# The S5 recurrence of a transformer block, computed in blocks of four time steps instead of step by step

## The chip, the core and the metric

The kernel runs on one core of one Trainium2 chip. Five engines work side by side from queues of their own: TensorE (PE; its weight loads are shown as PEld), VectorE (DVE), ScalarE (ACT), GpSimd (POOL) and SyncE (SP), which here issues the DMAs. They wait for each other through semaphores. TensorE's clock is granted by a throttle at one of two levels, 1.2 and 2.4 GHz; the profile shows the share granted. The metric is the device time of one execution in microseconds, the median of several runs.

## What is computed

A sequence of 512 tokens of width 1024 goes through a first block (differential attention of 8 heads, an S5 state-space branch, gates, a convolutional feed-forward part) and then through four further mixers with feed-forward parts. The change is in the S5 branch alone, in the first tenth of the time. Cut to what matters:

```python
SSM_GROUP = 16; SSM_GROUPS = 32; SSM_STATE = 64          # 512 channels in 32 groups, 64 complex states each
def s5_layer(u, ...):                                    # u: seq x 512
    lb = mag * (cos + i sin)                             # one complex factor per group and state
    bb = c * b                                           # 64 x 16 complex, per group
    bu = einsum('blgc,gpc->blgp', u, bb)
    x[l] = lb * x[l-1] + bu[l]                           # associative scan over the 512 steps
    y = einsum('gcp,blgp->blgc', c_re, x_re) - einsum('gcp,blgp->blgc', c_im, x_im) + d_skip * u
    g = gelu(y)
    return g * sigmoid(g @ w_glu + b_glu)
```

## The kernel before

Matrices are feature-major: channels on the 128 partitions, the 512 tokens along the row. Every projection runs as three matmuls on float32 parts rounded to a shorter type (`wh`, `wl`, `hh`, `hl`). A weight block comes by DMA into `raw` (L230), ACT rounds it into `wh` (L236) and DVE, for some POOL, takes the rest into `wl` (L237); two `raw` buffers take turns, so the next load is issued when the block before has been read.

The S5 channels u are four tiles of 128 channels. `SSM.run(q, ...)` handles one of them and goes through four smaller tiles i = 4q + j of 32 channels (2 groups, 2 x 64 = 128 states on partitions). For each:

- `tables(i)` builds the cosine and sine of the angle at each of 512 steps by doubling (L1033 to L1042): POOL copies 32 entries, then four doublings of 2 x 2 ACT products (L1040, L1041) and 2 POOL sums (L1042).
- Two float32 matmuls L1057 bring 32 channels to 128 states (32 rows of contraction, 512 columns), into the banks `br` and `bi`.
- Four DVE products L1060 and two POOL sums L1061, L1062 turn the states back by the tables, so that the complex recurrence becomes two real ones; two DVE scans L1065 run them over 512 steps; three DVE and one POOL product L1067 and two POOL sums L1068, L1069 turn the result forward again.
- Two float32 matmuls L1071 (32 output columns) put y into a quarter of bank 3. After the four tiles DVE adds the skip d * u (L1075) and writes the result over u.

Which instruction comes when is settled in two steps. The program is written as generators that `weave` takes in turn: in each of four passes p two attention heads (`heads`, from L874 to L900: scores, reduction L876, exponentials L877, a sum by L882, transposes L885, matmuls with v L889), a piece of the recurrence (4, 6 and 6 of its 16 steps in the passes 0 to 2), the projections of the next pair of heads (`pair`) and some of the 16 gate tiles (`gates`, each stored to DRAM by L1139; a head's result by L902). In the pass 3 GLU and sigmoids run in place of recurrence and projections. A scheduler then orders the instructions within that. Banks 0 to 2 serve projections and states, 3 is y, 4 the attention result, 5 to 7 scores and transposes. The GLU reads u token by token.

Of the kernel before, what the change touches and what calls it, by code (L numbers as in the profile page):

```python
# [12 lines left out]
AF = mybir.ActivationFunctionType  # L13
# [27 lines left out]
def const_arrays():  # L41
# [11 lines left out]
    cols["half"] = ((p[:, None] // 16) % 2 == np.arange(P)[None, :] // 64)  # L53
# [852 lines left out]
class SSM:  # L906


    def __init__(self, K, are, aim):
# [14 lines left out]
        mag = self.mag = new("mag")  # L924
# [20 lines left out]
        tr = K.slot("trig")[:, 0:432].rearrange("p (a w i) -> p a w i", a=3, i=16)  # L945
        self.cw, self.sw, self.nsw = tr[:, 0], tr[:, 1], tr[:, 2]
# [4 lines left out]
        nc.gpsimd.tensor_scalar(out=self.nsw, in0=self.sw, scalar1=-1.0, scalar2=None, op0=ALU.mult)  # L951

        nr, ni, den, x, cr, ci = (new(m) for m in ("nr", "ni", "den", "x", "cr", "ci"))
        tt(nr, mag, self.cw[:, 0, :], ALU.mult)
        nc.gpsimd.tensor_scalar(out=nr, in0=nr, scalar1=-1.0, scalar2=None, op0=ALU.add)
        tt(ni, mag, self.sw[:, 0, :], ALU.mult)
# [19 lines left out]
        self.bb = []  # L976
        tmp = small()[:, 0:256].rearrange("p (i c) -> p i c", c=16)
        for x0, x1, op in ((b[0], b[1], ALU.subtract), (b[1], b[0], ALU.add)):
            bd = small()
            nc.gpsimd.memset(bd, 0.0)  # L980
            bv = bd.rearrange("p (i g c) -> p i g c", g=2, c=16)
            r = small()[:, 0:256].rearrange("p (i c) -> p i c", c=16)
            tt(r, x0, bc(cr), ALU.mult)
            tt(tmp, x1, bc(ci), ALU.mult)
            for g in range(2):
                s = slice(64 * g, 64 * g + 64)
                tt(bv[s, :, g, :], r[s], tmp[s], op)
            ps = K.psa()
            for q in range(4):
                nc.tensor.transpose(out=ps[:, q * P:(q + 1) * P], in_=bd[:, q * P:(q + 1) * P], identity=K.ident)  # L990
            self.bb.append(K.slot("bb"))
            nc.scalar.copy(out=self.bb[-1], in_=ps)

        self.cm = []
        hm = K.cload("half")
        for nm, sg in (("ssm_c_re", 1.0), ("ssm_c_im", -1.0)):
# [3 lines left out]
            half = hm.rearrange("p (g s) -> p g s", g=2).unsqueeze(1).to_broadcast([P, 4, 2, 64])  # L1000
            tt(rows, rows, half, ALU.mult)
# [1133 lines left out]
```

## Time and profile before

| | us |
|---|---|
| median of 3 runs | 3902.36 (3899.41 to 3907.14) |
| profiled execution, its own time | 3907.43 |
| its span | 3905.70 |
| busy: PE, DVE, ACT, POOL | 3749.0, 2596.6, 2078.7, 1380.1 |
| recurrence with attention | 104 to 472 |
| attention with GLU | 472 to 575 |

The page is one execution. Busy times are averages over stages with different limits, so a change is read from the stage it is in. A row of the windows view gives what each engine was busy in a stretch, the mean granted clock (1.00 is 2.4 GHz) and the DMA's share. Waits name the releaser that came last. A float32 matmul leaves two records in the trace; a transpose leaves one. Records of one group that follow each other overlap, so the length of one is read from the starts of its neighbours.

### The profile page before, as it was taken

The numbers are of one execution on the slowest core, as the hardware profiler recorded it, in microseconds if no ns is written. First come the engines' busy times: TensorE is split into PE (matmuls) and PEld (weight loads), VectorE is DVE, ScalarE is ACT, GpSimd is POOL, SyncE is SP. The second block draws the span as 40 slices with busy tenths as digits, with TensorE's granted clock in tenths as the row PEclk, the third lists the DMA queues.
The fourth block names the chain that finished last, engine by engine and source line by source line (L and its number), as shares of the span: only waits on it lengthen the run. The fifth ranks groups of instructions, "written<-read, shape, count | busy, mean of one in ns | idle before, by whom it ended". The sixth has DMA issues, their size and how long they took to land.

```text
span 3905.7 us, 51250 instructions
## 1 busy us (share of the span) xinstructions
PE 3749.0 (96%) x19014; PEld 3048.5 (78%) x19014; DVE 2596.6 (66%) x3960; ACT 2078.7 (53%) x3757; POOL 1380.1 (35%) x1358
## 2 busy tenths in 40 slices
PE   8999999999996999999999999999899999999998
PEld 7665678878876887898888888776777878788887
DVE  5678866665698765676676567457776566676545
ACT  4555664564644654476465446654556445554333
POOL 5567602343002543342454341255734340022000
PEclk9898899999998999999999999999999999999999
DMA  4111243555321454332245535342255531132231
GB/s 150 54 57 44 69 143 120 190 168 170 108 87 34 157 189 155 122 101 78 99 151 191 166 100 173 133 134 78 74 185 171 173 108 61 46 106 82 93 106 66
DMA packets 393431, 458.06 MB, mean 117 GB/s; under 512 B 35571, under 2 KB 307357, under 8 KB 393181
## 3 DMA queue, kind: packets, MB, share of 16 engines
q1 hardware_dynamic: 393181, 454.78, 35.9%
q8 instruction: 150, 2.46, 0.3%
q14 instruction: 100, 0.82, 0.1%
HBM read 421.56 MB, written 33.03 MB: 116 GB/s over the span
## 4 chain that ended last, share of the span: by engine, by line
PE 74%; DVE 11%; POOL 6%; DMA 3%; ACT 3%; issue 2%; SPq 0%; DVEq 0%; POOLq 0%; ACTq 0%
PE bank L251 20%; PE bank L254 20%; PE bank L255 20%; DMA mix<-in_ada_w_dram 3%; DVE wl L237 2%; PE bank L1906 1%; POOL mix L585 1%; DVE cacc L1300 1%; PE bank L1071 1%; PE bank L1914 1%; ACT mix L583 1%; PE bank L317 1%; PE bank L319 1%; PE bank L318 1%; PE bank L874 1%
## 5 line engine op out<-in xcount | busy, mean ns | idle before, releaser
L251 PE MATMUL bank<-hh,wh 128*128 128x512 f32 (+1 forms) x2928 | 1101.0, 377 | 12.5 <-ACT hh L244 5.3
L254 PE MATMUL bank<-hh,wl 128*128 128x512 f32 (+1 forms) x2928 | 1095.0, 375 | 4.1 <-DVE wl L237 4.1
L255 PE MATMUL bank<-hl,wh 128*128 128x512 f32 (+1 forms) x2928 | 1090.0, 376 | 4.0 <-DVE hl L247 3.4
L237 DVE TENSOR_TENSOR wl<-raw,wh 128x1024 fp32r<-128x1024 f32 (+2 forms) x524 | 668.6, 1277 | 205.9 <-ACT wh L236 199.7
L236 ACT CAST wh<-raw 128x1024 fp32r<-128x1024 f32 (+1 forms) x550 | 562.5, 1026 | 390.9 <-PE bank L255 338.2
L585 POOL TENSOR_TENSOR mix<-mix,mix 128x512 f32<-128x512 f32 x336 | 501.3, 1492 | 757.1 <-ACT mix L583 740.2
L251 PEld LDWEIGHTS bank<-hh,wh 128*128 128x128 f32 x2928 | 557.4, 190 | 126.5 <-ACT hh L244 8.7
L254 PEld LDWEIGHTS bank<-hh,wl 128*128 128x128 f32 x2928 | 556.8, 190 | 111.4 <-DVE wl L237 6.8
L255 PEld LDWEIGHTS bank<-hl,wh 128*128 128x128 f32 x2928 | 551.8, 190 | 114.6 <-DVE hl L247 4.5
L583 ACT ACTIVATE mix<-mix,cs 128x512 f32<-128x512 f32 x384 | 270.6, 722 | 296.9 <-DMA mix<-in_ada_w_dram 295.4
L667 DVE SCALAR_TENSOR_TENSOR mix<-bank,vl,mix 128x510 f32<-128x510 f32 (+3 forms) x384 | 268.6, 700 | 205.2 <-ACT mix L328 197.1
L254 PE MATMUL bank<-uh,wl 128*128 128x512 f32 (+1 forms) x1008 | 371.0, 368 | 3.6 <-DVE wl L237 3.6
L251 PE MATMUL bank<-uh,wh 128*128 128x512 f32 (+1 forms) x1008 | 370.5, 368 | 0.0
L255 PE MATMUL bank<-ul,wh 128*128 128x512 f32 (+1 forms) x1008 | 369.9, 367 | 0.0
L624 DVE SCALAR_TENSOR_TENSOR X<-bank,M,X 128x512 f32<-128x512 f32 (+1 forms) x192 | 120.6, 635 | 238.5 <-PE bank L255 238.2
L254 PEld LDWEIGHTS bank<-uh,wl 128*128 128x128 f32 x1008 | 189.5, 188 | 39.4 <-DVE wl L237 5.4
L251 PEld LDWEIGHTS bank<-uh,wh 128*128 128x128 f32 x1008 | 189.5, 188 | 35.1
L255 PEld LDWEIGHTS bank<-ul,wh 128*128 128x128 f32 x1008 | 189.5, 188 | 34.1
L328 ACT ACTIVATE mix<-bank,vl 128x512 f32<-128x512 f32 (+1 forms) x192 | 141.1, 735 | 86.3 <-PE bank L255 86.2
L244 ACT CAST uh<-mix 128x512 fp32r<-128x512 f32 x110 | 68.0, 618 | 174.3 <-DVE mix L694 173.9
L247 DVE TENSOR_TENSOR ul<-mix,uh 128x512 fp32r<-128x512 f32 x110 | 95.8, 871 | 75.6 <-ACT uh L244 75.1
L358 POOL TENSOR_TENSOR qs<-qs,sq 128x256 f32<-128x256 f32 (+1 forms) x88 | 106.7, 1214 | 54.1 <-ACT sq L343 53.5
(810 smaller groups left out, 7067.1 us busy)
## 6 DMA issues: line engine op xcount, KB each, us to landing
mix<-in_ada_w_dram SPq DMA_DIRECT2D x384, 256.0 KB
raw<-in_ffn_w_up_dram SPq DMA_DIRECT2D x88, 1024.0 KB
raw<-in_ffn_w_down_dram SPq DMA_DIRECT2D x32, 1024.0 KB
raw<-in_w_in_dram SPq DMA_DIRECT2D x22, 1024.0 KB
raw<-in_w_up_dram SPq DMA_DIRECT2D x22, 1024.0 KB
raw<-in_hg_w_in_dram SPq DMA_DIRECT2D x16, 1024.0 KB
raw<-in_ml_w_up_dram SPq DMA_DIRECT2D x16, 1024.0 KB
raw<-in_cc_w_pw_dram SPq DMA_DIRECT2D x12, 1024.0 KB
```

Of the source, the lines that this page charges most:

```text
L236: nc.scalar.copy(out=h, in_=src)
L237: eng.tensor_tensor(out=l, in0=src, in1=h, op=ALU.subtract)
L247: nc.vector.tensor_tensor(out=lo, in0=src, in1=hi, op=ALU.subtract)
L251: i = mm(out=out, lhsT=wh, rhs=xh, start=start, stop=False)
L254: mm(out=out, lhsT=wl, rhs=xh, start=False, stop=False)
L255: return mm(out=out, lhsT=wh, rhs=xl, start=False, stop=stop)
L328: self.nc.scalar.activation(out=dst[:, o:o + w], in_=ps, func=func, **kw)
L358: self.qadd.tensor_tensor(out=self.qs[:, c], in0=self.qs[:, c], in1=q[:, c], op=ALU.add)
L583: nc.scalar.activation(out=o, in_=o, func=AF.Copy, scale=self.cs[:, k:k + 1])
L585: nc.gpsimd.tensor_tensor(out=acc, in0=acc, in1=o, op=ALU.add)
L624: self.nc.vector.scalar_tensor_tensor(out=x, in0=ps, scalar=gate[:, n:n + 1], in1=x, op0=ALU.mult, op1=ALU.add)
L667: nc.vector.scalar_tensor_tensor(out=d, in0=ps[:, :n - s], scalar=col(s), in1=d, op0=ALU.mult, op1=ALU.add)
```

## The change

The recurrence takes four time steps at once: x[4n+3] from x[4n-1], with the four inputs of a block side by side. For each q, a new `prepare` has 16 DMAs of 32 partitions x 128 elements (L1073, 16 KB) move u inside SBUF so that partition 32k + c holds step k of channel c for tile j, 128 blocks along the row. u itself is stored with k outermost (`natural`). The tables need 128 entries instead of 512, for four tiles at once, and are doubled by DVE (`double`). `powers` multiplies B and C by the powers of the factor on DVE, a half of the partitions at a time; the B powers are transposed (L1080).

`run` then makes, for all four tiles, 8 matmuls L1103 of 128 x 128 x 128, DVE products and sums of 512 columns (L1105 to L1107), two scans (L1110) that cover the four tiles in one row (`rho` holds a zero between them), the turn forward (L1112 to L1114), all on DVE. The terms inside a block come from 16 small matmuls L1124 (copied by ACT into `taps`, L1127); 12 matmuls of 128 or 127 columns (L1131, L1133) give y, ACT copies it from the bank (L1135), 16 DMAs (L1138) take it back into the layout of u, and the skip (L1140) waits for them. The buffers `uw`, `bb`, `cs`, `bd`, `cd`, `taps`, `rho` and `work` are there once. Half masks and the transposes of B in the constructor go, some memsets come. Lines of the changed kernel are one lower than before up to about L920, and 68 higher behind the class.

```diff
-    def tables(self, i):
-
-        K = self.K
-        g = K.nc.gpsimd
-        C, S, tmp = self.tab[i % 2]
-        g.tensor_copy(out=C[:, 0:32], in_=self.c32[:, i, :])
-        g.tensor_copy(out=S[:, 0:32], in_=self.s32[:, i, :])
-        for lev in range(5, 9):
-            w = 2 ** lev
-            c, s, ns = (v[:, lev, i:i + 1] for v in (self.cw, self.sw, self.nsw))
-            for dst, u0, u1, k in ((C, C, S, ns), (S, S, C, s)):
-                o = dst[:, w:2 * w]
-                K.nc.scalar.activation(out=tmp[:, 0:w], in_=u1[:, 0:w], func=AF.Copy, scale=k)
-                K.nc.scalar.activation(out=o, in_=u0[:, 0:w], func=AF.Copy, scale=c)
-                g.tensor_tensor(out=o, in0=o, in1=tmp[:, 0:w], op=ALU.add)
-        return C, S
...
+        f = small.t + [K.tmp("vrow"), K.rings["sq"].t[0], K.rings["mix"].t[9]]
+        self.work, self.cs, self.rho, self.tmp = f[0:4], f[4:6], f[6], f[7]
+        self.taps, self.bb, self.uw = f[8], f[9:11], f[11]
+        self.bd, self.cd = ([K.slot(n) for _ in range(2)] for n in ("bd", "cd"))
+        self.c0 = K.slot("c0")
+        for t in (*self.bd, *self.cd, self.c0, self.taps, self.rho):
+            nc.gpsimd.memset(t, 0.0)
...
+    def tables(self, q):
+
+        tiles = slice(4 * q, 4 * q + 4)
+        C, S = (x.rearrange("p (j n) -> p j n", n=P) for x in self.cs)
+        for o, x in ((C, self.c32), (S, self.s32)):
+            self.K.nc.scalar.copy(out=o[:, :, 0:32], in_=x[:, tiles, :])
+        tmp = self.tmp[:, 0:256].rearrange("p (j n) -> p j n", n=64)
+        for lev in (5, 6):
+            self.double(C, S, tiles, lev, tmp, self.K.nc.vector)
+
+    def powers(self, src, q, k0, conj, dst):
+
+        tt = lambda o, x, y, op: self.K.nc.vector.tensor_tensor(out=o, in0=x, in1=y, op=op)
+        tiles = slice(4 * q, 4 * q + 4)
+        t0, t1 = (self.tmp[:, o:o + 256].rearrange("p (j k c) -> p j k c", k=4, c=16) for o in (0, 256))
...
+        for d, x0, x1, op in ((dst[0], re, im, sub), (dst[1], im, re, add)):
+            dv = d.rearrange("p (j k g c) -> p j k g c", k=4, g=2, c=16)
+            tt(t0, x0, lr, ALU.mult)
+            tt(t1, x1, li, ALU.mult)
+            for g in range(2):
+                s = slice(64 * g, 64 * g + 64)
+                tt(dv[s, :, :, g, :], t0[s], t1[s], op)
+
+    def prepare(self, q, u):
+        K, nc = self.K, self.K.nc
+        for j in range(4):
+            for k in range(4):
+                nc.sync.dma_start(out=self.uw[32 * k:32 * k + 32, j * P:(j + 1) * P],
+                                  in_=u[q][32 * j:32 * j + 32, k * P:(k + 1) * P])
+        self.tables(q)
+        self.powers(self.B, q, 1, False, self.bd)
+        for x in range(2):
+            ps = K.psa()
+            for j in range(4):
+                nc.tensor.transpose(out=ps[:, j * P:(j + 1) * P], in_=self.bd[x][:, j * P:(j + 1) * P], identity=K.ident)
+            nc.scalar.copy(out=self.bb[x], in_=ps)
+        self.powers(self.C, q, 0, True, self.cd)
+        c0 = self.c0[:, 0:256].rearrange("p (x j g c) -> p x j g c", x=2, g=2, c=16)
+        for g in range(2):
+            s = slice(64 * g, 64 * g + 64)
+            nc.gpsimd.tensor_copy(out=c0[s, :, :, g, :], in_=self.C[s, :, 4 * q:4 * q + 4])
+        nc.scalar.copy(out=self.rho.rearrange("p (j n) -> p j n", n=P)[:, :, 1:P],
+                       in_=self.mag4[:, 4 * q:4 * q + 4].unsqueeze(2).to_broadcast([P, 4, P - 1]))
 
     def run(self, q, u, dcol):
...
-        v, g = nc.vector, nc.gpsimd
+        v = nc.vector
         mm = nc.tensor.matmul
+        self.prepare(q, u)
+        yield
+        part = [slice(j * P, (j + 1) * P) for j in range(4)]
+        t, (C, S) = self.work, self.cs
+        br, bi = bank = [K.psm(), K.psm()]
+        for x, pb in enumerate(bank):
+            for c in part:
+                mm(out=pb[:, c], lhsT=self.bb[x][:, c], rhs=self.uw[:, c], start=True, stop=True)
+        for o, x0, x1 in ((t[0], br, C), (t[1], bi, S), (t[2], bi, C), (t[3], br, S)):
+            v.tensor_tensor(out=o, in0=x0, in1=x1, op=ALU.mult)
+        v.tensor_tensor(out=t[0], in0=t[0], in1=t[1], op=ALU.add)
+        v.tensor_tensor(out=t[2], in0=t[2], in1=t[3], op=ALU.subtract)
+        yield
+        for o, x in ((t[1], t[0]), (t[3], t[2])):
+            v.tensor_tensor_scan(out=o, data0=self.rho, data1=x, initial=0.0, op0=ALU.mult, op1=ALU.add)
+        for o, x0, x1 in ((t[0], C, t[1]), (t[1], S, t[1]), (t[2], C, t[3]), (t[3], S, t[3])):
+            v.tensor_tensor(out=o, in0=x0, in1=x1, op=ALU.mult)
+        v.tensor_tensor(out=t[0], in0=t[0], in1=t[3], op=ALU.subtract)
+        v.tensor_tensor(out=t[2], in0=t[2], in1=t[1], op=ALU.add)
+
+        ps = K.psa()
+        p4 = ps.rearrange("p (j k c) -> p j k c", k=4, c=32)
+        c0 = self.c0[:, 0:256].rearrange("p (x j c) -> p x j c", x=2, c=32)
+        bd, cd = ([x.rearrange("p (j k c) -> p j k c", k=4, c=32) for x in y] for y in (self.bd, self.cd))
+        for j in range(4):
+            for o, w in ((p4[0:32, j, 0:3, :], [x[:, j, 1:4, :] for x in cd]),
+                         (p4[0:32, j, 3, :], [c0[:, x, j, :] for x in range(2)])):
+                for x in range(2):
+                    mm(out=o, lhsT=bd[x][:, j, 3, :], rhs=w[x], start=x == 0, stop=x == 1, tile_position=(0, 0))
+        taps = self.taps.rearrange("p (j k c) -> p j k c", k=4, c=32)
+        for k in range(4):
+            nc.scalar.copy(out=taps[32 * k:32 * k + 32, :, 0:4 - k, :], in_=p4[0:32, :, k:4, :])
+        yield
         y = K.bank["y"]()
+        for j, c in enumerate(part):
+            mm(out=y[:, c], lhsT=self.taps[:, c], rhs=self.uw[:, c], start=True, stop=False)
+            for x, s in ((0, t[0]), (1, t[2])):
+                mm(out=y[:, j * P + 1:(j + 1) * P], lhsT=self.cd[x][:, c], rhs=s[:, j * P:(j + 1) * P - 1], start=False,
+                   stop=x == 1)
+        nc.scalar.copy(out=t[1], in_=y)
         for j in range(4):
-            i = 4 * q + j
-            C, S = self.tables(i)
-            r = slice(32 * j, 32 * j + 32)
-            br, bi = K.psm(), K.psm()
-            for x, pb in enumerate((br, bi)):
-                mm(out=pb, lhsT=self.bb[x][r, q * P:(q + 1) * P], rhs=u[q][r, :], start=True, stop=True)
-            t = self.work[i % 2]
-            for o, x0, x1 in ((t[0], br, C), (t[1], bi, S), (t[2], bi, C), (t[3], br, S)):
-                v.tensor_tensor(out=o, in0=x0, in1=x1, op=ALU.mult)
-            g.tensor_tensor(out=t[0], in0=t[0], in1=t[1], op=ALU.add)
-            g.tensor_tensor(out=t[2], in0=t[2], in1=t[3], op=ALU.subtract)
-            rho = self.mag[:, i:i + 1].to_broadcast([P, T])
-            for o, x in ((t[1], t[0]), (t[3], t[2])):
-                v.tensor_tensor_scan(out=o, data0=rho, data1=x, initial=0.0, op0=ALU.mult, op1=ALU.add)
-            for e, o, x0, x1 in ((v, t[0], C, t[1]), (v, t[1], S, t[1]), (v, t[2], C, t[3]), (g, t[3], S, t[3])):
-                e.tensor_tensor(out=o, in0=x0, in1=x1, op=ALU.mult)
-            g.tensor_tensor(out=t[0], in0=t[0], in1=t[3], op=ALU.subtract)
-            g.tensor_tensor(out=t[2], in0=t[2], in1=t[1], op=ALU.add)
-            for x, s in ((0, t[0]), (1, t[2])):
-                mm(out=y[r, :], lhsT=self.cm[x][:, q * P + 32 * j:q * P + 32 * j + 32], rhs=s, start=x == 0, stop=x == 1,
-                   tile_position=(0, 32 * j))
-            if j < 3:
-                yield
-        v.scalar_tensor_tensor(out=u[q], in0=u[q], scalar=dcol[:, q:q + 1], in1=y, op0=ALU.mult, op1=ALU.add)
+            for k in range(4):
+                nc.sync.dma_start(out=t[3][32 * j:32 * j + 32, k * P:(k + 1) * P],
+                                  in_=t[1][96 - 32 * k:128 - 32 * k, j * P:(j + 1) * P])
+        v.scalar_tensor_tensor(out=u[q], in0=u[q], scalar=dcol[:, q:q + 1], in1=t[3], op0=ALU.mult, op1=ALU.add)
...
+    natural = lambda x: x.rearrange("p (k n) -> p n k", k=4)
+    blocks = lambda x: x.rearrange("p (n k) -> p n k", k=4)
...
-        K.act(u[-1], K.feat(blk[n // 2], n % 2, K.Hh, K.Hl, HALF if n < 2 else FULL))
+        for ps, o, w in K.feat(blk[n // 2], n % 2, K.Hh, K.Hl, HALF if n < 2 else FULL):
+            nc.scalar.copy(out=natural(u[-1])[:, o // 4:(o + w) // 4, :], in_=blocks(ps))
...
-            K.split(x, gh[-1], gl[-1])
+            K.split(natural(x), blocks(gh[-1]), blocks(gl[-1]))
...
-                nc.vector.tensor_tensor(out=s, in0=s, in1=u[q], op=ALU.mult)
+                nc.vector.tensor_tensor(out=blocks(s), in0=blocks(s), in1=natural(u[q]), op=ALU.mult)
```

On SyncE, where the gate tiles of the passes 0 and 1 are stored (`gd`), head results (`od`), and weight blocks loaded (`raw`). Before:

```order
L1139 DMA gd_1709<-out 128x512
L902 DMA od_1092<-mix_100 128x512
L230 DMA raw_75<-in_w_in_dram 128x8x256
L1139 DMA gd_1770<-out 128x512
L1139 DMA gd_1918<-mix_100 128x512
L230 DMA raw_75<-in_w_in_dram 128x8x256
L230 DMA raw_74<-in_w_in_dram 128x8x256
```

And after, the same stretch:

```order
L901 DMA od_1099<-mix_100 128x512
L1207 DMA gd_1746<-out 128x512
L1073 DMA mix_101<-u 32x128 x7
L1138 DMA hf_85<-hf_89 32x128 x16
L1073 DMA mix_101<-u 32x128 x2
L1207 DMA gd_1879<-mix_100 128x512
L1073 DMA mix_101<-u 32x128 x7
L229 DMA raw_75<-in_w_in_dram 128x8x256
L229 DMA raw_74<-in_w_in_dram 128x8x256
```

The return of q = 0 and the input of q = 1 now stand between the gate store and two weight loads.

On DVE, around the skip of q = 0 that ends its step. Before:

```order
L876 TENSOR_REDUCE st_121<-bank_72 128x1
L237 TENSOR_TENSOR wl_83<-raw_75,wh_79 128x1024
L879 RECIPROCAL st_121<-st_121 128x2
L1075 SCALAR_TENSOR_TENSOR u<-u,vm_129,bank_69 128x512
L880 TENSOR_TENSOR st_121<-st_121,nlam_557 128x1
L882 SCALAR_TENSOR_TENSOR mix_98<-mix_99,st_121,mix_98 128x512
```

And after:

```order
L1054 TENSOR_TENSOR qs_103<-ssmC,trig 128x256
L1054 TENSOR_TENSOR cd<-qs_103 64x16x16 x2
L1054 TENSOR_TENSOR qs_103<-ssmB,trig 128x256
L1140 SCALAR_TENSOR_TENSOR u<-u,vm_129,hf_85 128x512
L875 TENSOR_REDUCE st_121<-bank_71 128x1
L236 TENSOR_TENSOR wl_83<-raw_75,wh_79 128x1024
L875 TENSOR_REDUCE st_121<-bank_72 128x1
```

The skip read a bank of TensorE; now it reads `hf_85`, which the DMAs write, and the reductions of a head's scores stand behind it.

On PE, in the stretch of the first passes. Before, between the scores of two heads:

```order
L874 MATMUL bank_71<-kT,qT 128x256
L875 MATMUL bank_71<-maskr,identr 128x128
L1057 MATMUL bank_67<-u,bb 128x512
L1057 MATMUL bank_68<-u,bb 128x512
L1071 MATMUL bank_69<-hf_87,cm 32x512
L1071 MATMUL bank_69<-qs_103,cm 32x512
L874 MATMUL bank_73<-kT,qT 128x384
L875 MATMUL bank_73<-maskr,identr 128x128
```

And after, the states of q = 0:

```order
L873 MATMUL bank_71<-kT,qT 128x384
L874 MATMUL bank_71<-maskr,identr 128x128
L1103 MATMUL bank_67<-mix_101,vrow_124 128x128 x4
L1103 MATMUL bank_68<-mix_101,sq_90 128x128
L873 MATMUL bank_72<-kT,qT 128x384
L874 MATMUL bank_72<-maskr,identr 128x128
L1103 MATMUL bank_68<-mix_101,sq_90 128x128 x2
```

Pieces of 512 columns and 32 rows or 32 output columns have become pieces of 128 columns.

## Rows read from the trace of the kernel before

**Rows 1.** The page: granted clock of TensorE in 40 slices, in tenths

```profile
PEclk9898899999998999999999999999999999999999
```

**Rows 2.** Windows: start:end length, busy PE PEld DVE ACT POOL, clock, DMA, GB/s

```profile
104.00:472.00 368.00, 345.20 (x1604) 233.32 (x1603) 288.05 (x418) 204.18 (x544) 242.09 (x269) 0.87 0.16 51
472.00:575.00 103.00, 102.04 (x445) 75.04 (x445) 64.66 (x115) 73.85 (x147) 7.26 (x8) 1.00 0.45 146
```

**Rows 3.** Waits in 104 to 472: who waits <- for whom: us, times, longest

```profile
PE bank L874 <- ACT mix L877: 5.8, 3, 3.8
...
ACT wh L236 <- PE bank L255: 16.2, 2, 9.0
...
SPq L230 <- DVE wl L237: 120.8, 8, 28.3
```

**Rows 4.** Windows of the 13 half-clock stretches (two shown), and their sum

```profile
100.30:103.71 3.41, 3.41 (x19) 3.41 (x18) 0.75 (x2) 0.53 (x3) 3.33 (x7) 0.50 0.48 138
...
427.98:438.22 10.24, 6.39 (x10) 2.24 (x11) 10.24 (x16) 3.71 (x13) 10.24 (x11) 0.50 0.44 128
...
sum 102.41, PE 90.49 PEld 54.12 DVE 77.93 ACT 49.83 POOL 72.39; mean PE 6.96 PEld 4.16 DVE 5.99 ACT 3.83 POOL 5.57
```

**Rows 5.** PE groups just before a fall, 103.71 to 107.12: busy us, mean ns

```profile
L1057 PE MATMUL bank<-u,bb 32*128 32x512 f32 x4 | 2.2, 640 | 0.0
```

**Rows 6.** Timeline of PE at full clock: start us, length us, instruction

```profile
226.82 1.05 PE L1071 MATMUL bank<-vrow,cm 128*32 128x512 f32 x2
...
228.66 0.38 PE L292 MATMUL bank<-wh,hl 128*128 128x256 f32 x1
...
232.44 1.98 PE L1057 MATMUL bank<-u,bb 32*128 32x512 f32 x4
...
234.35 0.66 PE L885 MATMUL bank<-cst,mix 128*128 128x128 f32 x4
234.77 0.37 PE L290 MATMUL bank<-wh,hh 128*128 128x256 f32 x1
...
238.39 1.05 PE L889 MATMUL bank<-head,v 128*128 128x128 f32 x8
...
239.19 0.37 PE L290 MATMUL bank<-wh,hh 128*128 128x256 f32 x1
```

**Rows 7.** DVE groups in 100 to 475: busy us, mean ns | idle before

```profile
L1065 DVE TENSOR_TENSOR_SCAN sq<-mag,vrow 128x512 f32<-128x512 f32 x8 | 14.2, 1772 | 2.8 <-POOL vrow L1061 2.8
...
L880 DVE TENSOR_TENSOR st<-st,nlam 128x1 f32<-128x1 f32 x24 | 11.2, 465 | 0.3
L1060 DVE TENSOR_TENSOR sw<-bank,hf 128x512 f32<-128x512 f32 x16 | 10.6, 678 | 0.0
...
L1065 DVE TENSOR_TENSOR_SCAN sw<-mag,sw 128x512 f32<-128x512 f32 x8 | 9.9, 1243 | 0.0
...
L1067 DVE TENSOR_TENSOR hf<-hf,vs 128x512 f32<-128x512 f32 x8 | 7.8, 972 | 0.0
...
L1067 DVE TENSOR_TENSOR sw<-hf,sw 128x512 f32<-128x512 f32 x8 | 5.4, 680 | 0.0
...
L876 DVE TENSOR_REDUCE st<-bank 128x1 f32<-128x256 f32 x13 | 5.4, 412 | 7.4 <-PE bank L875 7.4
...
L876 DVE TENSOR_REDUCE st<-bank 128x1 f32<-128x128 f32 x12 | 3.4, 282 | 20.3 <-PE bank L875 20.3
```

**Rows 8.** Groups by line in 0 to 800, POOL's table sums

```profile
L1042 POOL TENSOR_TENSOR hf<-hf,hf 128x32 f32<-128x32 f32 (+3 forms) x128 | 81.5, 639 | 73.2 <-ACT hf L1040 73.1
```

**Rows 9.** DVE groups in 475 to 600, behind the recurrence

```profile
L880 DVE TENSOR_TENSOR st<-st,nlam 128x1 f32<-128x1 f32 x8 | 1.2, 154 | 0.1
```

**Rows 10.** Timeline far later: a DMA inside SBUF, and its reader

```profile
3483.79 0.49 SPq L1921 DMA_DIRECT2D vrow<-vs  x1
...
3486.08 0.43 DVE L246 CAST o<-vrow 128x512 fp32r<-128x512 f32 x1 [4.95 <-DMA vrow<-vs]
```

More of the change, by code (lines that the diff above doesn't have):

```diff
@@ L923, in __init__ @@
         new = lambda n: K.col([P, 16], n)
-        mag = self.mag = new("mag")
+        mag = new("mag")
         tt(mag, are, dt, ALU.mult)
@@ L950, in __init__ @@
         nc.gpsimd.tensor_scalar(out=self.cw, in0=self.cw, scalar1=-2.0, scalar2=1.0, op0=ALU.mult, op1=ALU.add)
[L951 to L956, printed above, removed]
+        lam = tr[:, 288:448].rearrange("p (x k i) -> p x k i", x=2, i=16)
+        lr, li = self.lr, self.li = lam[:, 0], lam[:, 1]
+        nc.gpsimd.memset(lr[:, 4, :], 1.0)
+        nc.gpsimd.memset(li[:, 4, :], 0.0)
+        mk = mag
+        for w, k in enumerate((1, 2, 4)):
+            if w:
+                m2 = new(f"mag{k}")
+                tt(m2, mk, mk, ALU.mult)
+                mk = m2
+            tt(lr[:, 4 - k, :], mk, self.cw[:, w, :], ALU.mult)
+            tt(li[:, 4 - k, :], mk, self.sw[:, w, :], ALU.mult)
+        self.mag4 = mk
+        x = new("x")
+        for o, u0, u1, op in ((lr, lr, li, ALU.subtract), (li, li, lr, ALU.add)):
+            tt(x, u1[:, 2, :], li[:, 3, :], ALU.mult)
+            tt(o[:, 1, :], u0[:, 2, :], lr[:, 3, :], ALU.mult)
+            tt(o[:, 1, :], o[:, 1, :], x, op)
+        nr, den, cr, ci = (new(m) for m in ("nr", "den", "cr", "ci"))
+        ni = li[:, 3, :]
+        nc.gpsimd.tensor_scalar(out=nr, in0=lr[:, 3, :], scalar1=-1.0, scalar2=None, op0=ALU.add)
         tt(den, are, are, ALU.mult)
@@ L975, in __init__ @@
         bc = lambda v: v.unsqueeze(2).to_broadcast([P, 16, 16])
-        self.bb = []
         tmp = small()[:, 0:256].rearrange("p (i c) -> p i c", c=16)
[L978 to L983, printed above, removed]
-            tt(tmp, x1, bc(ci), ALU.mult)
[L985 to L996, printed above, removed]
+        self.B = K.slot("ssmB").rearrange("p (x i c) -> p x i c", x=2, c=16)
+        for x, (x0, x1, op) in enumerate(((b[0], b[1], ALU.subtract), (b[1], b[0], ALU.add))):
+            tt(self.B[:, x], x0, bc(cr), ALU.mult)
+            tt(tmp, x1, bc(ci), ALU.mult)
+            tt(self.B[:, x], self.B[:, x], tmp, op)
+        self.C = K.slot("ssmC").rearrange("p (x i c) -> p x i c", x=2, c=16)
+        for x, (nm, sg) in enumerate((("ssm_c_re", 1.0), ("ssm_c_im", -1.0))):
             rows = small().rearrange("p (q g s) -> p q g s", q=4, g=2)
@@ new lines, in double @@
+    def double(self, C, S, tiles, lev, tmp, eng):
+        tt = lambda o, x, y, op: eng.tensor_tensor(out=o, in0=x, in1=y, op=op)
+        w, n = 2 ** lev, tiles.stop - tiles.start
+        cw, sw = (v[:, lev + 2, tiles].unsqueeze(2).to_broadcast([P, n, w]) for v in (self.cw, self.sw))
+        A, B = C[:, :, 0:w], S[:, :, 0:w]
+        for dst, u0, u1, op in ((C, A, B, ALU.subtract), (S, B, A, ALU.add)):
+            o = dst[:, :, w:2 * w]
+            tt(tmp[:, :, 0:w], u1, sw, ALU.mult)
+            tt(o, u0, cw, ALU.mult)
+            tt(o, o, tmp[:, :, 0:w], op)
```

31 lines of the change are left out of this document (12 added, 19 removed).

## The prediction

> **What bounds the kernel now.** I read the page's slices first, then stages, waits and single instructions. The granted clock of TensorE (PEclk) stands at 8 tenths in three of the first five slices and once more in all the rest, else at 9 or more [rows 1]. The SSM recurrence, woven with attention heads and gate projections, fills 104 to 472 us. In that stage PE is busy 345.2 of 368 us, DVE 288, POOL 242, and the mean granted clock is 0.87 [rows 2]. In the 103 us behind it, with the same attention and no recurrence, POOL is busy 7.26 us, PE 102.04 and the clock is 1.00 [rows 2]. So PE sets the pace here: a matmul taken away shortens the stage unless something else comes late. PE's longest wait is for the exponentials of the softmax, 5.8 us in three pieces. Casts of weights (L236) wait until PE is done with an earlier tile, not for data, and SyncE holds weight loads back until DVE has freed a buffer (120.8 us): the loads come early [rows 3].
>
> The missing 0.13 of the clock is 13 stretches at 0.50, 1.2 instead of 2.4 GHz, together 102.41 us [rows 4]; by the stage's mean the loss is (1 − 0.87) × 368 = 48 us. In the longest ones DVE and POOL are full and PE is not: 10.24, 10.24 and 6.39 of 10.24 us [rows 4]. In 9 of the 13, the matmuls that feed the recurrence (L1057, 32 rows of contraction) run in the few microseconds just before the fall, as here [rows 5].
>
> **The change part by part.** The profiled execution took 3907.43 us (span 3905.70); the median of the runs is 3902.36, 5 us lower. I work from the profiled one and take 5 off.
>
> *TensorE work.* At full clock four L1057 records take from 232.44 to 234.35, 1.91 us, 0.48 each; four L1071 records from 226.82 to 228.66, 1.84, 0.46 each [rows 6]. A float32 matmul leaves two records. Sixteen tiles of 32 channels make 64 of each: 64 × 0.48 + 64 × 0.46 = 60 us. Now a block of four steps is contracted at once, and columns fall from 512 to 128. The rows for that size are 8 records of L889 in 0.80 us, 0.10 each, and 4 transposes in 0.42 us, 0.105 each [rows 6]. Per group of 128 channels there are 8 matmuls L1103 (16 records, 1.6 us), 8 transposes (0.84), 16 matmuls for the taps L1124 of 96 or 32 columns (32 records, between half of 0.10 and all of it, 1.6 to 3.2) and 12 matmuls into y (24 records, 2.4): 6.5 to 8 us, four times 26 to 32. Eight transposes of the constructor go (0.8). Taking 30 added, the term is **−30**, between −28 and −34.
>
> *DVE and POOL.* Before, DVE spends 64 × 0.68 on L1060 (one of eight like groups shown), 45.9 on the scans (four groups, dearest and cheapest shown), 39 on L1067 (six groups, the same) and 3 on L1075: 131.5 us [rows 7]. After, per q: 12 products and sums of 512 columns at 0.68, 2 scans at 1.24 in place of 8, 6 table steps of 128 elements at 0.28, 22 table and power steps of 256 elements at 0.41 (the two reductions of that width [rows 7]) and the final step, 0.75: 22.1 us, four times 88. So 43 us go. POOL keeps two small copies per q: its table sums L1042 (81.5 us in 128 pieces [rows 8]) and its 512-wide sums end. That matters for DVE, which pays beside a busy POOL: the one-column step L880 takes 465 ns in the stage and 154 behind it [rows 7, 9]. DVE should fall from 288 to about 205. None of this is PE time, so it counts only through the next two terms.
>
> *Clock.* Two things that stand around the falls go, the runs of 32-row matmuls and the full DVE and POOL. Bounds are none of the 48 us and all of them. Attention has 64-row matmuls too, and the stage behind keeps 1.00 with them, but it has no token projections between; I take two thirds: **−32**.
>
> *PE idle.* 22.8 us of the stage. With DVE less full the softmax comes sooner; behind the stage only 0.96 of 103 us is idle, which in proportion leaves 3.4. I take **−8**, between 0 and −15.
>
> *New waits.* Two groups of 16 DMAs per q: the input u into blocks (L1073), and y back (L1138). The nearest row is a move inside SBUF of 64 x 512: issued at 3483.79 in 0.49 us, read by DVE at 3486.08, 2.3 us later [rows 10]. A group is then 16 × 0.49 = 7.8 us of issuing and 2.3 of landing: 10.1 us; in two waves, since in the built program each DMA waits for the one eight before it, 12.4. The input group stands far ahead of its matmuls, except that its buffer comes free only after the previous q's y; the PE rows between (about 209 of them behind q0's y, 95 behind q1's) hide it. The return group is tight. DVE's L1140 waits for it, and in q0 it stands eight DVE rows behind the last power, some 6 us after y; the softmax reductions of the next head (L876, in the new file L875) are queued behind it. So 10.1 − 6 = 4 us of stopped DVE in q0, and the same in q3, where little stands between: **+8**. The floor is 0 (other matmuls cover it); the ceiling is four groups of 12.4 with one cover of 6, +44. On SyncE two weight loads now stand behind up to 32 small DMAs, 32 × 0.49 = 16 us; loads issued early [rows 3] cover that, and without the cover it would be 16 us once or twice.
>
> The Trainium skill, "DMA: Bandwidth & Descriptors", sections "Anatomy of one DMA" and "Rules for kernel authors", speaks against this edit: each DMA has a fixed cost of about 2.0 us, and below 64 KB one pays mostly overhead. The 2.3 us of the row agree with it for one DMA. If the cost were paid 128 times in a row it would be an estimated 256 us; the sum above has it once a group, which no row of this case shows for a group of 16.
>
> *Constructor, GLU.* Seven memsets and small products come, half-mask products and the 8 transposes go; the GLU reads u through a stride on DVE, which has room there. Taken as 0, within 4 either way.
>
> Sum: −30 − 32 − 8 + 8 = −62. 3907.43 − 62 − 5 = **3840 us**.
>
> **The rivals.** *B, the clock stays low.* Attention's own gaps and 64-row matmuls could hold it, since 4 of the 13 falls had no L1057 before them. Then −30 − 8 + 8 = −30: 3872 us. *C, all of it comes back.* No falls, idle down by 15, returns hidden: −30 − 48 − 15 = −93: 3809 us. For it speaks the stage behind, with its 1.00 [rows 2]. *D, slower: the small DMAs of a group land one after another.* Then a group takes 16 × 2.3 = 37 us; DVE stands at L1140 for 37 − 6 = 31 us with the softmax behind it, and PE runs out of heads. Taking it three of four times (in one, projections fill the gap), +93 − 62 = +31: 3933 us. It decides from 62/3 + 6 = 27 us for a return group. Against it: 16 DMAs have 10 us to overlap, and nothing in the trace shows one waiting for another of its size. *E, no change:* the saved columns fall into gaps that the new waits open, 3902, within 8 us either way. PE's 94% [rows 2] speaks against it.
>
> **How the numbers follow.** Forecast A (3815 to 3870) 0.52, B 0.18, C 0.14, E 0.06, D 0.10. 0.2% is about 8 us, what a measurement of this kernel can tell from no change. Faster A + B + C = 0.84, same 0.06, slower 0.10. The range goes from C with the PE term at its lower bound and a few us of spread, 3800, to B with another 16 us of wait, 3888; it leaves out D, E and the tails of B and C, about 2 in 10.
>
> **What would show it.** The stage should end near 410 us instead of 472, with PE records of 128 columns at 0.10 us and PE columns for the recurrence near 30 us in place of 60. Stretches at 0.50 should sum to some 35 us; near 100 is B, near 0 is C. DVE should be busy near 205 us, and L880 near 0.2. L1140's wait for the return DMA should be about 4 us in q0; over 20 us at each q is D, and then the softmax reductions follow late and PE waits for L877. The time from the first L1138 issue to the L1140 should be 10 to 13 us. If a weight cast waits for a DMA, the queue on SyncE was read wrong. The prediction is wrong in kind if PE idle grows by more than the 30 us that are saved, whatever the clock does.

## The result, and the profile after

The changed kernel takes 3832.22 us (median of 4 runs, 3828.03 to 3834.66) against 3902.16 before (4 runs); the ratio is 0.982, interval 0.9807 to 0.9832. It is 70 us faster; 62 were forecast from the sum, and 3840 us as the time.

The profiled execution has a span of 3826.3 us, 79.4 below that of before. The two executions lie at opposite ends of their runs (3907.43 is the slowest of before, 3828.03 the fastest of after), which is why the spans differ by 9 us more than the medians. The page's row of the granted clock, to be held against [rows 1]:

```profile
PEclk9999999999989999999999999999899999999999
```

The three slices at 8 among the first five are gone. To compare the stages I use the stretch from the first score matmul (L874, in the new file L873) to the start of the last head result (L900, L899); it is called the stage from here on, and a half-clock stretch in it is called a fall. Columns as in [rows 2]. Before:

```profile
99.10:569.20 470.10, 446.34 (x2048) 308.47 (x2049) 353.22 (x533) 278.27 (x694) 254.09 (x283) 0.89 0.22 70
```

After:

```profile
109.80:495.20 385.40, 374.44 (x2239) 300.92 (x2240) 275.10 (x554) 219.65 (x475) 46.20 (x45) 0.99 0.28 90
```

The stage is 84.7 us shorter. PE's idle time goes from 23.8 to 11.0, its busy time from 446.3 to 374.4. Of those 71.9 us the clock makes 41: before, TensorE was busy 90.49 us at half clock [rows 4], half of it lost; after, the stage has only these two stretches and 1.7 us at its end, together 8.5 us:

```profile
275.10:278.51 3.41, 3.41 (x15) 2.85 (x14) 2.98 (x6) 1.05 (x2) 0.00 (x0) 0.52 0.64 226
350.20:353.61 3.41, 3.35 (x16) 3.24 (x17) 2.08 (x10) 0.99 (x2) 1.68 (x3) 0.52 0.46 159
```

The other 31 us are work: with half-clock time counted half, TensorE is busy 401.1 us before and 370.2 after. But the stage begins at 109.80 instead of 99.10: the set-up is 10.7 us longer. So −84.7 + 10.7 = −74.0 at the end of attention, and the remaining −5.4 of the spans lie behind it, where nothing was changed (3905.7 − 569.2 = 3336.5 against 3826.3 − 495.2 = 3331.1). In the kernels below this last part lies between 3331 and 3347 us (most of them at 3331 to 3334, and 3362 where the GLU came late), with unchanged code there. Part of this spread is work that a late stage leaves behind it: where the stage holds 24 TensorE records fewer (x2215 and x2279 below), 43 us instead of 38.6 pass from the last head result to the first work of the next part (L585, L584). The rest is not explained; TensorE's instructions later on come in nearly the same order in the runs compared. So a total can carry a dozen microseconds that are not from the edit's own place, and I give the stage beside it each time. Each stage is one traced execution.

### The profile page after: what moved, and what is told of

Its sections match the earlier page's. It is cut to its first block, busy times and chain, and to the rows that moved or that the text cites. A ratio compares the mean times of both kernels' runs of the same rounds, so it can differ in the third digit from the quotient of the medians.

```text
span 3826.3 us, 51401 instructions
## 1 busy us (share of the span) xinstructions
PE 3678.0 (96%) x19198; PEld 3038.3 (79%) x19198; DVE 2522.2 (66%) x3984; ACT 2023.8 (53%) x3541; POOL 1180.5 (31%) x1140
## 4 chain that ended last, share of the span: by engine, by line
PE 82%; DVE 8%; POOL 3%; ACT 2%; DMA 2%; issue 1%; SPq 0%; DVEq 0%; POOLq 0%; ACTq 0%
PE bank L250 23%; PE bank L254 22%; PE bank L253 22%; DMA mix<-in_ada_w_dram 1%; DVE wl L236 1%; PE bank L1974 1%; PE bank L873 1%; DVE cacc L1368 1%; PE bank L289 1%; PE bank L290 1%; PE bank L291 1%; PE bank L316 1%; PE bank L318 1%; PE bank L317 1%; PE bank L1982 1%
## 5 line engine op out<-in xcount | busy, mean ns | idle before, releaser
L584 POOL TENSOR_TENSOR mix<-mix,mix 128x512 f32<-128x512 f32 x336 | 504.1, 1500 | 748.6 <-ACT mix L582 731.2
```

Of the source, the lines that this page charges most:

```text
L584: nc.gpsimd.tensor_tensor(out=acc, in0=acc, in1=o, op=ALU.add)
```

## The experiments

### What lowers the clock: 32-row matmuls, or a starved TensorE

Theory F: the 32-row matmuls of L1057 bring the falls. Rival W: DVE and POOL are full, TensorE is starved, and the clock falls for that. The first run puts matmuls of the old form back:

```diff
         for x, pb in enumerate(bank):
+            for j in range(4):
+                mm(out=pb, lhsT=self.bb[x][0:32, 0:P], rhs=self.uw[0:32, :], start=True, stop=True)
             for c in part:
```

> The changed kernel with 32 more float32 matmuls of the old form (32 rows of contraction, 512 columns; 8 ahead of each q's L1103, their results overwritten). Theory F, the 32-row matmuls bring the falls of the clock: 64 records x 0.48 = 31 us of columns, and the stretches at half clock in the recurrence's stage go from about 10 us to 50 to 100, which costs another 20 to 45: 3885 to 3910. Rival W, the falls come from DVE and POOL being full and TensorE starved: 31 us of columns alone, falls under 25 us, 3855 to 3870.

Measured: 3890.75 us (ratio 0.997, 0.9955 to 0.9985). The control has `self.bb[x][:, 0:P]` and `rhs=self.uw` instead, all 128 rows:

> The control: the same 32 matmuls with all 128 rows of contraction. Both theories: the same columns, 31 us, and falls under 25 us, 3855 to 3870. If falls come here as with 32 rows, it is the bunch of float32 matmuls and not their rows.

Measured: 3868.01 us (0.9909, 0.9894 to 0.9924). The stages, with 32 rows:

```profile
110.20:540.60 430.40, 425.32 (x2279) 324.60 (x2280) 276.92 (x550) 219.01 (x474) 47.03 (x44) 0.92 0.25 80
```

With 128 rows:

```profile
108.90:528.00 419.10, 405.64 (x2303) 314.49 (x2304) 280.99 (x555) 220.27 (x475) 46.19 (x45) 0.97 0.26 82
```

The control's stage is 33.7 us longer than the changed kernel's: with half-clock time counted half, 26.6 us of columns, 4.6 more of clock and 2.5 of idle time. With 32 rows PE is busy another 19.7 us at 0.92 of the clock instead of 0.97, although 24 records, nearly all of the projection behind attention (some 5 us), have not yet run in its stage, and it waits less than in any other run (5.1 us). The half-clock stretches sum to 68.3 us in seven falls, against 22.1 in three in the control. The first fall, with the 7 us before it, in which the eight records of the added matmuls ran:

```profile
135.20:142.20 7.00, 7.00 (x22) 3.47 (x21) 4.57 (x8) 2.23 (x4) 2.02 (x2) 1.00 0.50 156
142.20:166.10 23.90, 23.90 (x56) 13.61 (x56) 13.24 (x26) 5.40 (x13) 0.00 (x0) 0.50 0.16 54
```

TensorE was busy throughout, and in six of the seven falls it is so. So the form alone brings falls, with TensorE hardly idle; F is shown on this kernel. The gap of the totals is 22.7 us. In the stage it is 11.3, or some 16 with the 24 records; whether what lies behind the stage belongs to the price is not shown, so 11 to 23 us is what these runs allow.

The second suspect alone, POOL kept busy in the changed kernel:

```diff
         for o, x0, x1 in ((t[0], br, C), (t[1], bi, S), (t[2], bi, C), (t[3], br, S)):
-            v.tensor_tensor(out=o, in0=x0, in1=x1, op=ALU.mult)
+            d = v.tensor_tensor(out=o, in0=x0, in1=x1, op=ALU.mult)
+        for _ in range(12):
+            K.after(nc.gpsimd.tensor_tensor(out=self.dum, in0=self.dum, in1=self.dum, op=ALU.mult), d)
...
```

> The changed kernel with 96 POOL products of 512 columns on a tile of their own (24 per q, set behind DVE's products), about 130 us of POOL work, which nobody waits for. W: DVE slows beside them (the step L879 goes from 166 ns towards 465), falls of 30 to 80 us come back, 3845 to 3880. F: DVE slows, but falls stay under 25 us and the time stays within 10 us of 3832.

The same 12 stand behind the products L1112. Measured: 3874.59 us (0.9931, 0.9914 to 0.9948). Its stage:

```profile
107.80:529.30 421.50, 392.58 (x2229) 309.50 (x2230) 326.90 (x551) 220.27 (x475) 178.19 (x143) 0.94 0.26 82
```

And the one-column step on DVE, a group row of 100 to 500 us:

```profile
L879 DVE TENSOR_TENSOR st<-st,nlam 128x1 f32<-128x1 f32 x31 | 10.5, 338 | 0.5
```

Nobody waits for these products, and the stage still grows by 36.1 us: 18.0 of idle and 18.1 of busy time, with the clock at 0.94. DVE takes 327 us instead of 275, and the step that takes 166 ns in the changed kernel (row below, in the review) takes 338. From 100 to 530 us PE waits 23 us for DVE instead of 8, while DVE's own wait for the POOL sum L822 did not grow (6.0 us against 7.6). The half-clock stretches sum to 54.6 us in five falls. The third, with the 7 us before it:

```profile
278.40:285.40 7.00, 2.39 (x16) 1.82 (x15) 6.96 (x7) 1.02 (x4) 6.69 (x5) 1.00 0.05 11
285.40:305.90 20.50, 18.05 (x55) 11.39 (x53) 13.51 (x28) 6.20 (x17) 12.44 (x12) 0.50 0.36 126
```

DVE and POOL are full there, TensorE stands still for 4.6 of the 7 us, and then the clock falls; TensorE had stood for part of the 7 us before each of the five. So W is true as well: POOL work slows DVE, TensorE waits, and the clock falls behind the waits. The two theories were not exclusive, and the prediction's "two things that stand around the falls" both count.

### The same from the side of the kernel before

```diff
-            C, S = self.tables(i)
+            C, S = self.tables(i) if i < 2 else self.tab[i % 2][0:2]
```

> The kernel before with the tables built for the tiles 0 and 1 alone (14 of 16 builds left out): POOL loses about 14/16 of 95 us, ACT 14/16 of 99, the 32-row matmuls stay. F: the falls stay near 100 us in sum, time 3885 to 3902. W: the falls shrink to under half, time 3840 to 3875.

Measured: 3904.14 us (1.0002, 0.9991 to 1.0013), no change. The falls, 78.5 us, are neither near 100 nor under half of it, and the time is nearer F; but it is no clean test of W, since DVE is as busy as before (350.5 us in the stage below, against 353.2).

```diff
-                mm(out=pb, lhsT=self.bb[x][r, q * P:(q + 1) * P], rhs=u[q][r, :], start=True, stop=True)
+                mm(out=pb, lhsT=self.bb[x][:, q * P:(q + 1) * P], rhs=u[q], start=True, stop=True)
```

> The kernel before with L1057 contracting all 128 rows instead of 32 (the states then mix four tiles; the columns and everything else stay). Theory F: the falls in the stage go from 102 us to under 60, and the time by half of what goes, 3875 to 3890. If the falls came from DVE and POOL alone, they stay near 100 and the time stays 3898 to 3908.

Measured: 3913.12 us (1.0029, 1.0018 to 1.004): 0.3% slower, where F expected 12 to 27 us off. Both edits together:

> The kernel before with both edits that did nothing alone: L1057 on 128 rows, and tables for two tiles only. If the clock and the waits for DVE and POOL hold each other's gain back, the two together give it: falls in the stage under 45 us and idle no higher than before, 3860 to 3890. If the two are simply without effect, 3898 to 3912.

Measured: 3886.59 us (0.9967, 0.9955 to 0.9979). The stages: without tables,

```profile
100.70:563.10 462.40, 436.82 (x2037) 300.02 (x2038) 350.54 (x528) 210.76 (x468) 179.70 (x143) 0.92 0.21 70
```

with 128 rows,

```profile
100.40:571.50 471.10, 428.50 (x2034) 299.96 (x2035) 356.72 (x529) 277.48 (x692) 254.81 (x283) 0.92 0.21 69
```

with both.

```profile
100.20:548.20 448.00, 412.77 (x2038) 292.46 (x2039) 353.45 (x529) 208.99 (x468) 179.62 (x143) 0.96 0.22 73
```

The 128 rows do what F says to PE's busy time (446.3 to 428.5), but idle time grows from 23.8 to 42.6, and the stage stays at 471. The waits that grew most are for DVE and POOL, which did not get a microsecond less to do; in the waits of PE in 100 to 575 us (in the same order, they took 2.4, 5.8, 2.7 and 1.6 us before):

```profile
PE bank L885 <- DVE mix L882: 9.4, 6, 3.3
PE bank L874 <- ACT mix L877: 8.3, 5, 3.3
PE bank L833 <- DVE mix L826: 6.8, 3, 4.5
PE bank L1071 <- POOL vrow L1068: 5.7, 2, 3.2
```

That run's further loss of some 10 us lies behind the stage (3918.5 − 571.5 = 3347.0, against 3336.5) and is not from the edit's own place. Alone the two edits change the stage by −7.7 and +1.0 us, together by −22.1: more than their sum. TensorE and the engines that feed it were both close to the limit in the kernel before, and the change relieved both. Which of these engines counts is not told apart here: leaving out the tables takes 74 us off POOL, 68 off ACT and only 3 off DVE, and with both edits the idle time is still 35.2 us, not back at 23.8 as was expected.

The traces also sort the falls. The table gives their sum in the stage, their number, and in how many of them TensorE had been busy throughout the 7 us before (a length chosen for this table):

| kernel | half clock, us | falls | without idle time ahead |
|---|---|---|---|
| before | 102.4 | 13 | 8 |
| before, without tables | 78.5 | 9 | 5 |
| before, 128 rows | 78.5 | 10 | 0 |
| before, both edits | 37.5 | 6 | 0 |
| changed | 8.6 | 3 | 0 |
| changed, 32 rows added | 68.3 | 7 | 6 |
| changed, 128 rows added | 22.1 | 3 | 0 |
| changed, POOL kept busy | 54.6 | 5 | 0 |

In all 19 of the last column, 32-row matmuls ran in those 7 us. With 128 rows this kind is gone from the kernel before, but falls behind waits take its place, and so the edit alone brought nothing. The sorting has one exception in the runs further below: with the moves of u issued by ACT, one fall has no idle time ahead of it and 64-row score matmuls instead.

### The set-up

The set-up begins with the load of x, which SyncE issues in two halves. SyncE's rows before, the second half of x and the first load of B:

```profile
15.07 3.24 SPq L492 DMA_DIRECT2D xt<-in_x_dram  x4
...
39.09 0.38 SPq L973 DMA_DIRECT2D hf<-in_ssm_b_re_dram  x1
```

and after:

```profile
15.33 0.97 SPq L1004 DMA_DIRECT2D vs<-in_ssm_c_re_dram  x2
16.35 0.51 SPq L1004 DMA_DIRECT2D qs<-in_ssm_c_im_dram  x1
17.96 1.88 SPq L491 DMA_DIRECT2D xt<-in_x_dram  x4
...
46.70 0.38 SPq L990 DMA_DIRECT2D hf<-in_ssm_b_re_dram  x1
```

Before, the loads of C stood at 55 to 61 us; in the changed kernel the scheduler issues them at 15 to 20 us, three of the four ahead of the second half of x. That the changed constructor needs fewer buffers and so leaves them free earlier is the likely reason, which no run tests. The next run puts them behind the loads of B again:

```diff
-            nc.sync.dma_start(out=t, in_=a[nm][0]...)
+            bload = nc.sync.dma_start(out=t, in_=a[nm][0]...)
...
-                nc.sync.dma_start(out=rows[:, :, g, :], in_=a[nm][0]...)
+                K.after(nc.sync.dma_start(out=rows[:, :, g, :], in_=a[nm][0]...), bload)
```

> The changed kernel with the four loads of C (L1004) placed on SyncE behind the loads of B, as they stood before the change. Theory S1: these loads, at 15 to 20 us ahead of the second half of x, make the norm late (its exponent step 25.8 instead of 22 us, B loads 46.7 instead of 39.1), and with it all that follows: attention starts near 102 instead of 109.8 us, time 3822 to 3827. Rival S2: the 16 moves of u at 52 to 64 us hold the weight loads back: attention stays near 109, time 3828 to 3836.

Measured: 3826.27 us (0.9809, 0.9793 to 0.9826). The load of B is back at 39.87 us, and the stage starts at 103.70:

```profile
103.70:487.60 383.90, 373.13 (x2240) 299.62 (x2241) 275.40 (x554) 219.59 (x476) 48.12 (x46) 0.99 0.28 90
```

That is 6.1 us of the 10.7, and the median is 6 us below the changed kernel's; the intervals of the two ratios overlap, but the trace shows the place. In the six traces of the changed kernel and its variants with early C the stage starts at 107.8 to 110.3, in the four with late C at 102.5 to 103.7. S1 holds for the greater part. The median is the lowest of this study. With the moves of u (L1073) issued by ACT as well (`nc.scalar.dma_start`):

> The same with the 64 moves of u into blocks issued by ACT instead of SyncE. If they hold back weight loads in the set-up (S2), attention starts near 101 us and the time is 3815 to 3825, below the run before by 3 or more. If the loads' order alone was at fault (S1), this is the run before within 4 us; 16 x 0.6 us a group on ACT could cost up to 10 where ACT is waited for.

Measured: 3833.07 us (0.982, 0.9805 to 0.9834). The stage begins 1.2 us earlier still, which is all that S2 has to offer here, and is 10 us longer:

```profile
102.50:496.40 393.90, 378.37 (x2242) 302.97 (x2243) 281.41 (x556) 220.16 (x476) 53.36 (x50) 0.98 0.27 88
```

The last 3 to 5 us of the later start are not settled.

### What the moves cost

Without the return moves:

```diff
-        for j in range(4):
-            for k in range(4):
-                nc.sync.dma_start(out=t[3][32 * j:32 * j + 32, k * P:(k + 1) * P], in_=t[1][...])
-        v.scalar_tensor_tensor(out=u[q], ..., in1=t[3], ...)
+        v.scalar_tensor_tensor(out=u[q], ..., in1=t[1], ...)
```

> The changed kernel without the 64 moves that take y back (L1140 adds y in the blocks' layout, so the values go to wrong places). It gives the price of the return as it is. If DVE's stop of 10.4 us at L1140 in q = 0 and SyncE's 40 us of issuing cost TensorE nothing: 3825 to 3836, as the changed kernel. If the price runs in proportion to the run with four times as many (+54 us for 192 moves more): 18 us less, 3810 to 3818.

Measured: 3844.22 us (0.9857, 0.9839 to 0.9875), 12 us slower than with them, which neither side expected. The stage:

```profile
110.30:497.40 387.10, 374.97 (x2215) 300.71 (x2216) 278.15 (x551) 218.92 (x474) 46.17 (x44) 0.97 0.27 86
```

It is 1.7 us longer than the changed kernel's 385.4 with 24 records fewer in it, and 7 us more of it go to the clock (23.9 us of half clock instead of 8.6); the rest, 3842.8 − 497.4 = 3345.4 instead of 3331.1, is behind the stage, where those records and code that the edit does not touch stand. So leaving the return out shortened nothing, and no price of it shows in its place; why the run is slower is open. With each group of moves done four times (`for _ in range(4)` around the two loops):

> The changed kernel with each return group of 16 moves done four times (64 DMAs, about 40 us a group). DVE should stand at L1140 for some 35 to 40 us in q = 0. If DVE's stop is a loss for TensorE as rival D of the forecast has it (three of four groups, each some 30 us), PE idles 60 to 95 us more, 3890 to 3930. If TensorE has other matmuls to run meanwhile, the loss is under 30 us, 3832 to 3862.

Measured: 3886.05 us (0.9954, 0.9939 to 0.9968), 54 us more than the changed kernel and just below the first of the two ranges. The stage:

```profile
108.60:518.90 410.30, 380.67 (x2132) 296.78 (x2133) 265.46 (x529) 205.77 (x450) 46.88 (x45) 0.90 0.25 79
```

SyncE's timeline around the first group:

```profile
187.93 41.99 SPq L1139 DMA_DIRECT2D hf<-hf  x64
...
237.56 0.43 SPq L229 DMA_DIRECT2D raw<-in_w_in_dram  x1
```

The expected stop of DVE is not there: the scheduler put the skip (here L1141) behind other work, the first at 235.2 us. The price came in two other ways. SyncE held stores and weight loads for 42 us a group; idle time is 29.6 us and the clock 0.90, which makes the stage 25 us longer with 107 records fewer in it. And the last skip came at 471.3 instead of 386.5 us, so that the GLU, which needs all four, was not done when attention was: from the last head result to the first work of the next part (L585, L584) it takes 66.4 us instead of 38.6. So late returns have a price at four times the number of moves, but not by the mechanism of rival D: no stop of DVE with the softmax behind it shows.

The return by ACT instead of SyncE, on top of the late C loads:

> C loads late, and the return moves issued by ACT instead of SyncE, so that weight loads and stores do not stand behind them. If SyncE's queue is what the return costs: 3 to 10 us below the run with late C alone, 3816 to 3823. If it costs nothing there, ACT's 40 us of issuing can only add: 3826 to 3840.

Measured: 3861.08 us (0.9904, 0.9887 to 0.9921), 35 us more than with late C alone and more than either side expected. The stage:

```profile
103.40:527.60 424.20, 394.07 (x2242) 314.36 (x2243) 282.41 (x555) 219.70 (x476) 50.46 (x47) 0.93 0.26 81
```

ACT's timeline after the copy of y:

```profile
182.98 1.88 ACTq L1138 DMA_DIRECT2D hf<-hf  x3
186.47 0.48 ACT L886 COPY mix<-bank 128x384 f32<-128x384 f32 x1 [3.52 <-PE bank L884]
186.48 8.92 ACTq L1138 DMA_DIRECT2D hf<-hf  x13
195.44 0.65 ACT L1190 COPY v<-bank 128x256 f32<-128x256 f32 x2 [8.49 <-DMA hf<-hf]
```

In this stretch ACT does nothing else while it issues, 8.92 us long, and the softmax exponentials and the copies out of PSUM are ACT's: PE's two longest waits are for the exponentials (L876, 7.3 and 5.3 us), idle time is 30.1 us and the clock 0.93. And both groups by POOL:

> C loads late and both groups of moves issued by POOL, which has 46 us of work in the 385 us of the stage. If a move costs POOL about what it costs SyncE (0.6 us), the queue of SyncE is free and nothing else waits: 3816 to 3826. If POOL takes longer to issue, L1140 comes later: 3826 to 3850.

Measured: 3845.6 us (0.9865, 0.9849 to 0.988). POOL issues a group of 16 in 7.8 us against SyncE's 10.0, and still the stage is 20 us longer than with SyncE, idle 18.6 us, clock 0.95. The stage:

```profile
103.70:507.50 403.80, 385.23 (x2240) 309.84 (x2241) 280.58 (x556) 219.40 (x476) 109.50 (x177) 0.95 0.27 85
```

POOL's timeline in q = 0 and 1:

```profile
181.32 7.91 POOL L1073 DMA_DIRECT2D mix<-u  x16 [7.68 <-PE bank L1131]
189.23 7.82 POOL L1138 DMA_DIRECT2D hf<-hf  x16
```

What of this is POOL's own work made late, and what the other order of instructions, the run does not tell apart. Of the three engines SyncE, on which only loads and stores issued ahead of need stand behind the moves, was the best for them here.

## Why the prediction was right, step by step

**TensorE columns: −30 forecast, −31 measured.** The 31 is what is left of TensorE's busy time when the clock is taken out. The pieces that can be read came near the prices of [rows 6]. In the timeline of the changed kernel 8 records of L1103 take from 137.82 to 138.76, and the 32 of the taps from 173.79 to 175.73:

```profile
137.82 1.10 PE L1103 MATMUL bank<-mix,vrow 128*128 128x128 f32 x8
138.76 0.39 PE L1103 MATMUL bank<-mix,sq 128*128 128x128 f32 x2
...
173.79 0.52 PE L1124 MATMUL bank<-cd,bd 128*32 128x96 f32 x4
...
175.73 0.51 PE L250 MATMUL bank<-hh,wh 128*128 128x512 f32 x1
```

That is 0.117 us a record instead of 0.10, and 1.94 us for the taps, inside their bounds of 1.6 and 3.2.

**DVE.** The group rows (100 to 500 us) that answer to [rows 7]:

```profile
L1112 DVE TENSOR_TENSOR hf<-hf,hf 128x512 f32<-128x512 f32 x16 | 10.4, 682 | 0.0
L1110 DVE TENSOR_TENSOR_SCAN hf<-vs,hf 128x512 f32<-128x512 f32 x8 | 9.4, 1211 | 0.0
L1054 DVE TENSOR_TENSOR qs<-ssmC,trig 128x256 f32<-128x256 f32 x16 | 6.1, 417 | 0.1
L879 DVE TENSOR_TENSOR st<-st,nlam 128x1 f32<-128x1 f32 x32 | 5.3, 166 | 0.6
```

0.68, 1.24 and 0.41 us were taken and 0.682, 1.211 and 0.417 came; the one-column step fell from 465 to 166 ns, as POOL went quiet. DVE is 78 us less busy in the whole stage (353 to 275); about 83 were forecast, of which the prediction worked out 43 and gave no sum for the rest.

**Clock: −32 forecast, −41 measured.** The step chose two thirds of 48 us because attention's own gaps might hold the clock; they did not. This term was mis-sized, and it is the largest part of the stage's surprise. The half-clock stretches of the stage sum to 8.6 us where the prediction named 35 as its sign and near 0 as that of rival C, which was the nearer one for the stage (no falls, idle down by 15 against 12.8 measured). The mechanism stands: 32-row matmuls and a starved TensorE each bring falls when put back alone. But the reading behind the second suspect was thin. "In the longest ones DVE and POOL are full" holds for the row shown; in the longest of all, 107.12 to 120.78, DVE was busy 6.92 and POOL 6.91 of 13.66 us, and over all 13 DVE was busy 76% of the time, no more than in the stage (288 of 368).

**PE idle: −8 forecast, −12.8 measured.** The proportion from the stage behind gave −19 and was cut to −8; the truth lay between.

**New waits: +8 forecast, none found.** Here the length was too small and the price too large. The rows around the first return, on the timeline of DVE and SyncE:

```profile
191.40 0.43 DVE L1054 TENSOR_TENSOR qs<-ssmB,trig 128x256 f32<-128x256 f32 x1
202.22 0.75 DVE L1140 SCALAR_TENSOR_TENSOR u<-u,vm,hf 128x512 f32<-128x512 f32 x1 [10.40 <-DMA mix<-u]
...
189.15 10.01 SPq L1138 DMA_DIRECT2D hf<-hf  x16
```

And the same stretch as windows:

```profile
188.75:195.58 6.83, 6.83 (x56) 6.66 (x55) 2.89 (x8) 1.47 (x4) 0.00 (x0) 1.00 0.11 26
195.58:202.41 6.83, 6.83 (x31) 4.81 (x29) 0.19 (x1) 1.29 (x2) 0.00 (x0) 1.00 0.11 24
```

Sixteen issues take 10.0 us, 0.63 each instead of 0.49, and the group 13.1 us to the read (10.1 forecast, 12.4 in two waves). The row of L1140 names a move of the next q because both use the same semaphores; by the semaphore that the last return move raises, this move had landed at 201.48. DVE stood for 10.4 us in q = 0, not 4, and for 0.5 us in the three others together. But TensorE was busy in every one of these microseconds, at full clock, with projection matmuls in its queue. The wait's floor of 0 was the truth as far as these rows show: this stop of DVE of 10 us had cover. The Trainium skill, "DMA: Bandwidth & Descriptors", section "Anatomy of one DMA", gives a fixed cost of about 2.0 us a DMA, fitted on DMAs that GpSimd issues. In the trace fourteen of these sixteen, which SyncE issues, land 1.7 to 1.8 us after their issue begins and the last two after 3.4 and 2.9, but they overlap: the group pays that time once, behind the last issue, not sixteen times (16 x 2.0 would be an estimated 32 us against the 13.1 measured).

**Set-up: 0 forecast, +10.7 measured.** This is the step that failed: "Taken as 0, within 4 either way". It counted the constructor's instructions and not where its loads stand on SyncE. The four loads of C went from 55 to 61 us to 15 to 20, three of them ahead of the second half of x, and 6.1 of the 10.7 us came back when they were put behind the loads of B; the other 4.6 are not explained.

Errors of both signs make the total come near: −23 in the stage's four terms (−85 against −62), +11 in the set-up, some more behind and between executions. That the median of 3832 comes so near to 3840 is luck in part; the way and the mechanisms of the stage are not.

## What to carry to other kernels

When several engines are close to their limit, an edit that relieves one may show nothing in the time, and two such edits more than their sum, as in the kernel before; look at idle time and clock together, since here the one was traded for the other. Small DMAs in groups cost here their issue on the queue and one landing, so put them on an engine whose other work has been issued ahead of need, not on one that others wait for. When an edit frees buffers, look at which loads the scheduler now issues earlier, and what they stand ahead of.

## What was not expected of the hardware

Matmuls of 32 rows of contraction lowered the granted clock (0.92 against 0.97 for the same matmuls with 128 rows), although TensorE was idle for only 5.1 of 430 us; in six of seven falls it had not stood still in the 7 us before. And the engine that issues a move pays for it by kind: 10.0 us for 16 on SyncE, 7.8 on POOL, 0.6 to 0.7 us each on ACT, which did nothing else in that time.
